# Attention of eight pairs of heads: the second half of two pairs instead of three is computed last, and the last output row block ends in a piece of 128 columns

## The chip, the cores and the metric

The kernel runs on one core of a Trainium2 chip. The engines are TensorE (PE, with its weight loads as PEld), VectorE (DVE), ScalarE (ACT), GpSimd (POOL) and SyncE (SP, here only a DMA queue). The metric is the device time of one execution in microseconds. Before the change three runs took 1085.05, 1080.59 and 1086.14 us (median 1085.05), and the profiled execution took 1081.32 us, of which 1078.8 us are the span that the profile shows.

## The reference

A decoder trunk of two layers runs on one sequence of 1024 tokens of width 1024. The even layer mixes an RWKV-7 and a gated MLP part; the change does not touch it. The odd layer is sliding-window attention and takes the last third of the time:

```
# odd layer, 16 heads of 64, 2 key/value heads, window 128, blocks of 128 queries
h  = modulate(rmsnorm(x), c)                 # adaLN
q, k, v, z = split(h @ W_in)
S  = -(q k^T)/8 + alibi                      # a block sees itself and the block before
P  = softmax with one learned sink per head
o  = P @ v
y  = o * silu(z)
x  = x + gate(c) * (y @ W_out)
out = rmsnorm(x)                             # the final norm
```

## The kernel before

Tokens are split into two halves of 512 (HT) and eight blocks of 128 (NB); heads go in eight pairs, n = 0 to 7 (KC = 8). A product of float32 matrices is made of three matmuls on a high and a low part of each side (hi·hi, hi·lo, lo·hi); a projection of 512 tokens is 24 matmuls of 512 columns into a PSUM tile `pproj`, of which there are two.

For each pair, `head_projs(n)` projects the queries (`qproj`, L1365: two casts on ACT, L1373, and two on DVE, L1374) and the gate z (`zgate`, L1358: tanh on ACT, L1362, and the product on DVE, L1363, into `y`). Pairs 0 to 5 project both halves there; for pairs 6 and 7 the second halves come last, at the end of `head_projs(7)`, in the order q of 7, z of 7, q of 6, z of 6.

`attend(n, half, Q, bias)` runs four iterations, one for each block of 128 queries. An iteration has four score matmuls (`pS`, L130), the bias and minimum on DVE (L1320), the exponentials on ACT (L1324), the reciprocal (DVE L1326), a fold of the two windows (POOL L1329), the scaling (ACT L1331), two transposes (PE L1334, `pT`), the high part (ACT L1337, `PH`) and low part (DVE L1338, `PL`) of the transposed probabilities, a causal mask on each (L1341: POOL for PH, DVE for PL), and four matmuls with the values (`po`). For every two iterations ACT (L1351, L1352) and DVE (L1353, L1354) combine the heads, and POOL multiplies into `y` (L1356).

The loop over pairs attends both halves of a pair for n < N1 (5), and only the first half for the others. After the loop, the second halves that were kept follow in the order 5, 7, 6. The program puts attention at a high priority, and a scheduler at build time then lays out one fixed order for each engine; the engines run their orders by themselves and wait for each other by semaphores. The queries of the kept second halves live in buffers of their own (tag QL, six of them), the others in tag Q (seven), which later holds the rows `gate` and `xr` too.

`wo_load(n)` (L1392) brings one half of the output weight's columns in eight chunks: a DMA on SP into one of three buffers `wraw` (L1398), the high part on ACT (`hi`, L1399), the low part on POOL or DVE in turn (`lo`, L1400). The first half is loaded before the last four projections, the second after the loop.

The tail adds the gate rows (`gate` + `gateb`, DVE L1439, both brought by DMAs on ACT's queue, L1433), and then for each block of 128 tokens splits y (`yh` ACT L1445, `yl` DVE L1446), multiplies by the weight in pieces of 512 columns (24 matmuls each into `pproj`), multiplies by the gate (DVE L1458), adds x (DVE L1459), squares and sums (ACT L1460), and after all pieces takes the root on POOL (L1466) and scales and writes the rows (L1469 to L1474). The last block has three pieces, `cuts`, and multiplies by the final norm's factor (L1462) piece by piece.

Of the kernel before, what the change touches and what calls it, by code (L numbers as in the profile page):

```python
# [11 lines left out]
F32 = mybir.dt.float32  # L12
# [8 lines left out]
P = 128  # L21
D = 1024
T = 1024
KC = 8
HT = 512
NB = 8
# [79 lines left out]
def tile_kernel(ctx, tc, x, cons, par, rows, ada, ada0, ew, wup, sgw, sgb, ewo, ow, owo, out, dbg=None):  # L106
# [25 lines left out]
    def transpose(out, in_, ident):  # L132
        clock[0] += 512 / 2400.0
        return nc.tensor.transpose(out, in_, ident)  # L134
# [131 lines left out]
    def proj(w, h, half):  # L266
        whi, wlo = w
        hhi, hlo = h[half]
        pt = pproj("pproj")
        for k in range(KC):  # L270
            mm(pt, lhsT=whi[:, k, :], rhs=hhi[:, k, :], start=(k == 0), stop=False)
            mm(pt, lhsT=whi[:, k, :], rhs=hlo[:, k, :], start=False, stop=False)
            mm(pt, lhsT=wlo[:, k, :], rhs=hhi[:, k, :], start=False, stop=(k == KC - 1))
        return pt
# [260 lines left out]
    gated = dp.tile([2, D], F32, name="gated")  # L535
# [565 lines left out]
    x1d = dp.tile([T, D], F32, name="x1d")  # L1101
# [142 lines left out]
    def p1(tag):  # L1244
        return ps.tile([P, HT], F32, name="p" + tag, tag=tag, bufs=2)
# [4 lines left out]
    at = ctx.enter_context(tc.tile_pool(name="at", bufs=1, side="right", reuse_waits="tile"))  # L1250
# [9 lines left out]
    for half in range(2):  # L1260
        sl = slice(half * HT, (half + 1) * HT)
# [13 lines left out]
    for half in range(2):  # L1275
        vt = at.tile([P, HT], F32, name="vt", tag="zth", bufs=2)
        S.activation(vt, proj(done["w9"], h, half) if half else done["v0"], AF.Copy, scale=0.5)  # L1277
        pt = p1("T")
        for i in range(4):
            transpose(pt[:, i * P:(i + 1) * P], vt[:, i * P:(i + 1) * P], ident)  # L1280
        p5 = pt.rearrange("p (b g d) -> p b g d", b=4, g=2)
        vb = slice(half * 4, half * 4 + 4 - half)
        for g in range(2):
            S.activation(VV[:, vb, g, 0, :], p5[:, 0:4 - half, g, :], AF.Copy)
            V.tensor_tensor(out=VV[:, vb, g, 1, :], in0=p5[:, 0:4 - half, g, :], in1=VV[:, vb, g, 0, :].bitcast(F32), op=ALU.subtract)
        vf = at.tile([P, 4, 2, 64], F32, name="vf", tag="QL", bufs=2 * (KC - 5))
        S.activation(vf, p5, AF.Copy)
        vfs.append(vf)
        dv = at.tile([P, 4, 2, 64], F32, name="dv", tag="QL", bufs=2 * (KC - 5))
        V.tensor_tensor(out=dv[:, 1:4], in0=p5[:, 1:4], in1=vf[:, 0:3], op=ALU.subtract)  # L1290
        i0 = 1 - half
        if half:
            V.tensor_tensor(out=dv[:, 0], in0=p5[:, 0], in1=vfs[0][:, 3], op=ALU.subtract)
        db = slice(half * 4 - 1 + i0, half * 4 + 3)
        S.activation(DV[:, db, :, 0, :], dv[:, i0:4], AF.Copy)
        G.tensor_tensor(out=DV[:, db, :, 1, :], in0=dv[:, i0:4], in1=DV[:, db, :, 0, :].bitcast(F32), op=ALU.subtract)

    N1 = 5

    def attend(n, half, Q, bias):  # L1300
        g = n // 4
# [63 lines left out]
    def qproj(n, w, half):  # L1365
        pt = proj(w, h, half)
        Q = []
        for e in range(2):
            a = slice(e * 64, e * 64 + 64)
            o = slice(64 - e * 64, 128 - e * 64)  # L1370
            tag, bufs = ("QL", 2 * (KC - N1)) if half and n >= N1 else ("Q", 7)
            q = at.tile([P, HT], F32R, name="Q", tag=tag, bufs=bufs)
            S.activation(q[a, :], pt[a, :], AF.Copy, scale=-0.125)  # L1373
            V.scalar_tensor_tensor(out=q[o, :], in0=pt[a, :], scalar=-0.125, in1=q[a, :].bitcast(F32), op0=ALU.mult, op1=ALU.subtract)  # L1374
            Q.append(q)
        qs[n, half] = Q
# [36 lines left out]
    for n in range(KC):  # L1413
        bias = biases(n)
        for half in range(2 if n < N1 else 1):
            with tc.high_priority(offset=BOOST):
# [4 lines left out]
    wo_load(1)  # L1421
    for n in (*range(N1, KC - 2), KC - 1, KC - 2):
        with tc.high_priority(offset=BOOST):
# [6 lines left out]
    def half_tiles(name, tag, bufs, src, dt=F32):  # L1430
        ts = [at.tile([P, HT], dt, name=name, tag=tag, bufs=bufs) for n in range(2)]
        for n in range(2):
            nc.scalar.dma_start(out=ts[n], in_=src(slice(n * HT, (n + 1) * HT)))  # L1433
        return ts

    gate = half_tiles("gate", "Q", 7, lambda ns: gated[1, ns].partition_broadcast(P))
    gb = half_tiles("gateb", "zth", 2, lambda ns: rows[1, ns].partition_broadcast(P))
    for n in range(2):
        V.tensor_tensor(out=gate[n], in0=gate[n], in1=gb[n], op=ALU.add)  # L1439
# [1 line left out]
    for b in range(NB):  # L1441
        sl = slice(b * P, (b + 1) * P)
# [1 line left out]
        yl = wp.tile([P, KC, P], F32R, name="yl", tag="wlo", bufs=2)  # L1444
        S.activation(yh, y[:, :, sl], AF.Copy)  # L1445
        V.tensor_tensor(out=yl, in0=y[:, :, sl], in1=yh.bitcast(F32), op=ALU.subtract)  # L1446
        xt = half_tiles("xr", "Q", 7, lambda ns: x1d[sl, ns])
        st = at.tile([P, 4], F32, name="st", tag="st", bufs=4)
        cuts = (0, HT, D) if b < NB - 1 else (0, HT, HT + 256, D)
        for i, (c0, c1) in enumerate(zip(cuts, cuts[1:])):  # L1450
            wh, wl = (w[:, :, c0 % HT:c0 % HT + c1 - c0] for w in wo[c0 // HT])
            xs_ = xt[c0 // HT][:, c0 % HT:c0 % HT + c1 - c0]
# [77 lines left out]
```

## Time and profile before

| what | us |
|---|---|
| median of three runs | 1085.05 |
| profiled execution | 1081.32 |
| its span | 1078.8 |
| odd layer's projections, from about | 738 |
| last projection's last matmul starts | 968.66 |
| first matmul of the output product | 974.20 |
| last matmul of the output product starts | 1071.52 |

In a row of the timeline stand the start, the length, engine, line, operation, output and inputs, and in brackets how long the engine was idle before it and what ended that. In a row of a group, behind the first bar, stand the busy time of all its instructions and the mean of one in ns, then the idle time before them. Starts of pipelined matmuls are the better clock: a matmul's length overlaps the next one.

### The profile page before, as it was taken

The page shows a single profiled execution, that of the slowest core. Times are in us where ns is not written, and L with a number is a line of the kernel's source. Part 1 is how long each engine was busy: PE and PEld are TensorE (multiplying, and loading weights), DVE is VectorE, ACT ScalarE, POOL GpSimd, SP SyncE. Part 2 cuts the span into 40 slices and gives each one's busy share as a digit, 9 for nine tenths or more (in the row PEclk, how much of TensorE's full clock was granted, in tenths as well). Part 3 has the DMA queues.
Part 4 walks back from the last instruction along what each step waited for, and adds up shares of the span by engine and source line. Part 5 has one row for each costly group of instructions (what it writes and reads, how often), then busy time and mean ns, then how long its engine had stood idle before and what let it go on. Part 6 is the DMA issues. An engine that isn't in the chain of part 4 may idle for free.

```text
span 1078.8 us, 20631 instructions
## 1 busy us (share of the span) xinstructions
PE 1031.4 (96%) x7776; PEld 824.6 (76%) x7776; DVE 714.6 (66%) x1727; ACT 551.8 (51%) x1383; POOL 405.5 (38%) x471
## 2 busy tenths in 40 slices
PE   6989999998999899999999999999999999999997
PEld 3657777777777777777888777878888888887886
DVE  4354948685868686867533588865767775688744
ACT  4464454545454646453514223336877786797221
POOL 2343323222333324232425100135666676688201
PEclk9999989999999999999999999999999999998999
DMA  9601221212132112121314454421110111332221
GB/s 363 241 18 39 65 74 40 81 49 69 52 99 67 60 50 80 57 71 58 107 47 154 146 181 152 165 77 40 40 40 21 40 40 39 120 111 84 101 95 69
DMA packets 55852, 94.53 MB, mean 88 GB/s; under 512 B 5829, under 2 KB 16197, under 8 KB 55753
## 3 DMA queue, kind: packets, MB, share of 16 engines
q1 hardware_dynamic: 45752, 78.41, 22.0%
q10 hardware_dynamic: 10000, 14.81, 4.5%
q8 instruction: 61, 1.00, 0.4%
q14 instruction: 39, 0.31, 0.1%
HBM read 80.61 MB, written 12.59 MB: 86 GB/s over the span
## 4 chain that ended last, share of the span: by engine, by line
PE 49%; DVE 4%; DMA 3%; ACT 2%; issue 1%; POOL 0%; POOLq 0%; ACTq 0%; DVEq 0%; SPq 0%
PE pproj L130 25%; PE op L130 14%; PE pS L130 2%; PE po L130 2%; PE pT L1334 1%; DMA araw<-ada 1%; DMA wraw<-owo 1%; PE htp L134 1%; PE pM L130 1%; DVE pr L728 1%; PE py L130 0%; DMA wraw<-y0d 0%; DVE adacc L944 0%; PE mix L130 0%; PE mq L130 0%
## 5 line engine op out<-in xcount | busy, mean ns | idle before, releaser
L130 PE MATMUL pproj<-hi,whi 128*128 128x512 f32 x696 | 282.5, 406 | 0.7 <-ACT vt L1277 0.7
L130 PE MATMUL pproj<-lo,whi 128*128 128x512 f32 x696 | 281.4, 404 | 0.0
L130 PE MATMUL pproj<-hi,wlo 128*128 128x512 f32 x696 | 281.3, 404 | 0.0
L258 POOL TENSOR_TENSOR wlo<-wraw,whi 128x512 fp32r<-128x512 f32 x90 | 121.2, 1364 | 145.5 <-ACT whi L257 145.4
L130 PEld LDWEIGHTS pproj<-hi,whi 128*128 128x128 f32 x696 | 131.8, 189 | 28.2 <-issue 4.0
L130 PEld LDWEIGHTS pproj<-hi,wlo 128*128 128x128 f32 x696 | 131.7, 189 | 26.4 <-issue 2.4
L130 PEld LDWEIGHTS pproj<-lo,whi 128*128 128x128 f32 x696 | 132.1, 190 | 25.2 <-issue 1.7
L130 PE MATMUL op<-wo,whi 128*128 128x512 f32 x256 | 81.1, 397 | 0.1
L257 ACT ACTIVATE whi<-wraw 128x512 fp32r<-128x512 f32 x106 | 61.3, 622 | 25.6 <-PE pproj L130 12.4
L1324 ACT ACTIVATE Sx<-Sx,nm 128x257 f32<-128x257 f32 (+1 forms) x128 | 62.1, 488 | 12.7 <-DVE nm L1320 12.3
L1320 DVE CUSTOM_DVE_ANT_0 Sx<-pS,bias,nsink 128x256 f32<-128x256 f32 (+1 forms) x128 | 53.1, 462 | 17.1 <-PE pS L130 14.2
L944 DVE SCALAR_TENSOR_TENSOR adacc<-araw,cond,adacc 128x512 f32<-128x512 f32 x56 | 48.3, 862 | 19.6 <-DMA araw<-ada 19.2
L130 PEld LDWEIGHTS op<-wo,whi 128*128 128x128 f32 x256 | 47.6, 188 | 11.3 <-ACT whi L257 0.5
L130 PE MATMUL op<-hi,yh 128*128 128x512 f32 (+1 forms) x136 | 52.4, 385 | 1.2 <-DVE y L1363 1.2
L1341 POOL TENSOR_TENSOR PH<-PH,causal 128x256 fp32r<-128x256 f32 x56 | 46.1, 825 | 18.9 <-ACT PH L1337 18.5
L130 PE MATMUL op<-hi,yl 128*128 128x512 f32 (+1 forms) x136 | 52.4, 385 | 0.0
L130 PE MATMUL op<-lo,yh 128*128 128x512 f32 (+1 forms) x136 | 52.3, 384 | 0.0
L130 PE MATMUL op<-wo,wlo 128*128 128x512 f32 x128 | 50.8, 397 | 0.0
L1331 ACT ACTIVATE Sx<-Sx,rc 128x128 f32<-128x128 f32 x128 | 43.7, 393 | 5.8 <-POOL Sx L1329 4.6
L1329 POOL TENSOR_TENSOR Sx<-Sx 128x256 f32<-128x256 f32 x56 | 42.2, 755 | 11.4 <-ACT Sx L1324 10.7
L225 POOL TENSOR_TENSOR st<-st,nhalf 128x1 f32<-128x1 f32 x16 | 9.6, 601 | 97.1 <-DVE st L224 97.1
L728 DVE TENSOR_TENSOR pr<-Lf,LT 128x2 f32<-128x2 f32 (+14 forms) x120 | 42.3, 353 | 2.4
(329 smaller groups left out, 2242.7 us busy)
## 6 DMA issues: line engine op xcount, KB each, us to landing
araw<-ada SPq DMA_DIRECT2D x64, 256.0 KB, 2.7
wraw<-ew SPq DMA_DIRECT2D x50, 256.0 KB, 3.0
wraw<-ow SPq DMA_DIRECT2D x40, 256.0 KB, 2.7
adaraw<-ada SPq DMA_DIRECT2D x16, 512.0 KB, 8.3
x<-x SPq DMA_DIRECT2D x8, 512.0 KB, 9.2
woraw<-ewo SPq DMA_DIRECT2D x16, 256.0 KB, 3.0
xr<-x ACTq DMA_DIRECT2D x16, 256.0 KB, 3.6
wraw<-y0d SPq DMA_DIRECT2D x16, 256.0 KB, 3.6
```

The lines of the kernel that those rows point to most:

```text
L130: last[0] = nc.tensor.matmul(out, lhsT=lhsT, rhs=rhs, **kw).ins
L134: return nc.tensor.transpose(out, in_, ident)
L257: a = S.activation(hi[:, gs, :], raws[g], AF.Copy)
L258: b = E.tensor_tensor(out=lo[:, gs, :], in0=raws[g], in1=hi[:, gs, :].bitcast(F32), op=ALU.subtract)
L728: V.tensor_tensor(out=pr[:, 0:nc_, 0:i + 1], in0=Lf[:, i:i + 1, 0:i + 1].to_broadcast([P, nc_, i + 1]), in1=LTt[:, 0:nc_, 0:i + 1], op=ALU ...
L944: op = V.scalar_tensor_tensor(out=acc, in0=raw, scalar=cond[:, k:k + 1], in1=acc, op0=ALU.mult, op1=ALU.add)
L1320: V.tensor_tensor_reduce(out=Sx[:, e, off:2 * P], in0=pS3[:, e, 0:nk], in1=bias[e][:, off:], scale=1.0, scalar=nsink[:, hd:hd + 1], op0=AL ...
L1324: S.activation(pr[:, e, off:2 * P + 1], Sx[:, e, off:2 * P + 1], AF.Exp, bias=nm[:, e:e + 1], scale=-1.0, accum_out=sm[:, e:e + 1])
L1329: G.tensor_tensor(out=F, in0=F, in1=pr[:, :, P:2 * P], op=ALU.add)
L1331: S.activation(F[:, e, :], F[:, e, :], AF.Copy, scale=rc[:, e:e + 1])
L1334: nc.tensor.transpose(pT[:, e * P:(e + 1) * P], F[:, e, :], ident)
L1341: E.tensor_tensor(out=pp_[:, 1, :].rearrange("p (e q) -> p e q", e=2), in0=pp_[:, 0, :].bitcast(F32).rearrange("p (e q) -> p e q", e=2), i ...
```

## The change

N1 goes from 5 to 6: pair 5's second half is attended in the loop and no longer kept, so two pairs (7, then 6) follow after the loop. Its queries take buffers of tag Q, which has one more, and tag QL has two fewer. In the last block of the tail, the three pieces are 512, 384 and 128 columns instead of 512, 256 and 256.

```diff
--- before.py
+++ after.py
@@ -1283,10 +1283,10 @@
         for g in range(2):
             S.activation(VV[:, vb, g, 0, :], p5[:, 0:4 - half, g, :], AF.Copy)
             V.tensor_tensor(out=VV[:, vb, g, 1, :], in0=p5[:, 0:4 - half, g, :], in1=VV[:, vb, g, 0, :].bitcast(F32), op=ALU.subtract)
-        vf = at.tile([P, 4, 2, 64], F32, name="vf", tag="QL", bufs=2 * (KC - 5))
+        vf = at.tile([P, 4, 2, 64], F32, name="vf", tag="QL", bufs=2 * (KC - 6))
         S.activation(vf, p5, AF.Copy)
         vfs.append(vf)
-        dv = at.tile([P, 4, 2, 64], F32, name="dv", tag="QL", bufs=2 * (KC - 5))
+        dv = at.tile([P, 4, 2, 64], F32, name="dv", tag="QL", bufs=2 * (KC - 6))
         V.tensor_tensor(out=dv[:, 1:4], in0=p5[:, 1:4], in1=vf[:, 0:3], op=ALU.subtract)
         i0 = 1 - half
         if half:
@@ -1295,7 +1295,7 @@
         S.activation(DV[:, db, :, 0, :], dv[:, i0:4], AF.Copy)
         G.tensor_tensor(out=DV[:, db, :, 1, :], in0=dv[:, i0:4], in1=DV[:, db, :, 0, :].bitcast(F32), op=ALU.subtract)
 
-    N1 = 5
+    N1 = 6
 
     def attend(n, half, Q, bias):
         g = n // 4
@@ -1368,7 +1368,7 @@
         for e in range(2):
             a = slice(e * 64, e * 64 + 64)
             o = slice(64 - e * 64, 128 - e * 64)
-            tag, bufs = ("QL", 2 * (KC - N1)) if half and n >= N1 else ("Q", 7)
+            tag, bufs = ("QL", 2 * (KC - N1)) if half and n >= N1 else ("Q", 8)
             q = at.tile([P, HT], F32R, name="Q", tag=tag, bufs=bufs)
             S.activation(q[a, :], pt[a, :], AF.Copy, scale=-0.125)
             V.scalar_tensor_tensor(out=q[o, :], in0=pt[a, :], scalar=-0.125, in1=q[a, :].bitcast(F32), op0=ALU.mult, op1=ALU.subtract)
@@ -1433,7 +1433,7 @@
             nc.scalar.dma_start(out=ts[n], in_=src(slice(n * HT, (n + 1) * HT)))
         return ts
 
-    gate = half_tiles("gate", "Q", 7, lambda ns: gated[1, ns].partition_broadcast(P))
+    gate = half_tiles("gate", "Q", 8, lambda ns: gated[1, ns].partition_broadcast(P))
     gb = half_tiles("gateb", "zth", 2, lambda ns: rows[1, ns].partition_broadcast(P))
     for n in range(2):
         V.tensor_tensor(out=gate[n], in0=gate[n], in1=gb[n], op=ALU.add)
@@ -1444,9 +1444,9 @@
         yl = wp.tile([P, KC, P], F32R, name="yl", tag="wlo", bufs=2)
         S.activation(yh, y[:, :, sl], AF.Copy)
         V.tensor_tensor(out=yl, in0=y[:, :, sl], in1=yh.bitcast(F32), op=ALU.subtract)
-        xt = half_tiles("xr", "Q", 7, lambda ns: x1d[sl, ns])
+        xt = half_tiles("xr", "Q", 8, lambda ns: x1d[sl, ns])
         st = at.tile([P, 4], F32, name="st", tag="st", bufs=4)
-        cuts = (0, HT, D) if b < NB - 1 else (0, HT, HT + 256, D)
+        cuts = (0, HT, D) if b < NB - 1 else (0, HT, D - P, D)
         for i, (c0, c1) in enumerate(zip(cuts, cuts[1:])):
             wh, wl = (w[:, :, c0 % HT:c0 % HT + c1 - c0] for w in wo[c0 // HT])
             xs_ = xt[c0 // HT][:, c0 % HT:c0 % HT + c1 - c0]
```

The orders of the engines are the same up to the z of pair 5's second half; from there pair 5's blocks 4 to 7 are spread between the last z of pair 5 and the queries of pair 7. SP's order is the same throughout.

On PE, the place where the last projection ends and the output product begins. `pproj` is the projection, `KH_7641` and `KL_7643` are the high and low part of the keys, `op` is the output product's first block. Before, its last rows and the first of the output product:

```order
L130 MATMUL po<-PH,DV 128x256
L1334 MATMUL pT<-con,Sx 128x128 x2
L130 MATMUL pS<-KH_7641,Q 128x256
L130 MATMUL pS<-KL_7643,Q 128x256
L130 MATMUL pS<-KH_7641,Q 128x256
L130 MATMUL pS<-KL_7643,Q 128x256
L130 MATMUL po<-PL,DV 128x256
L130 MATMUL po<-PH,VV 128x256
L1334 MATMUL pT<-con,Sx 128x128 x2
L130 MATMUL po<-PL,VV 128x256
L130 MATMUL po<-PH,DV 128x256
L130 MATMUL op<-hi,yh 128x512
```

The same place now; between the projection's last matmul and the first row stand four score matmuls:

```order
L130 MATMUL po<-PH,VV 128x256
L130 MATMUL po<-PL,VV 128x256
L1334 MATMUL pT<-con,Sx 128x128 x2
L130 MATMUL po<-PH,DV 128x256
L130 MATMUL pS<-KH_7641,Q 128x256
L130 MATMUL pS<-KL_7643,Q 128x256
L130 MATMUL pS<-KH_7641,Q 128x256
L130 MATMUL pS<-KL_7643,Q 128x256
L130 MATMUL op<-hi,yh 128x512
L130 MATMUL op<-lo,yh 128x512
L130 MATMUL op<-hi,yl 128x512
L130 MATMUL op<-hi,yh 128x512
```

Before, the iterations between the two are of pairs 5 and 7 (the fourth block of pair 5's second half and the first ones of pair 7's); now they are of pairs 7 and 6, and of the kept second halves eight iterations are left in all rather than twelve.

On DVE, from the split of y for the first block (`yl`) on. Before:

```order
L1446 TENSOR_TENSOR yl<-y_7630,yh 128x1024
L1338 TENSOR_TENSOR PL<-pT,PH 128x256
L1326 RECIPROCAL rc<-sm 128x2
L1439 TENSOR_TENSOR gate<-gate,gateb 128x512
L1363 SCALAR_TENSOR_TENSOR y_7630<-zth,pproj 128x512
L1341 TENSOR_TENSOR PL<-PL,causal 128x256
L1400 TENSOR_TENSOR lo<-wraw,hi 128x512
```

Now (the rows `Sx,nm` are the scores of pair 6, each with a read of its accumulator):

```order
L1446 TENSOR_TENSOR yl<-y_7630,yh 128x1024
L1320 ISA Sx,nm<-pS,bias,nsink 128x256
L1320 ISA nm 128x1
L1320 ISA Sx,nm<-pS,bias,nsink 128x256
L1320 ISA nm 128x1
L1320 ISA Sx,nm<-pS,bias,nsink 128x256
L1320 ISA nm 128x1
L1320 ISA Sx,nm<-pS,bias,nsink 128x256
L1320 ISA nm 128x1
L1363 SCALAR_TENSOR_TENSOR y_7630<-zth,pproj 128x512
L1439 TENSOR_TENSOR gate<-gate,gateb 128x512
L1400 TENSOR_TENSOR lo<-wraw,hi 128x512
```

The product of the last projection (`y_7630<-zth,pproj`) stood behind the gate sum, and now stands ahead of it; the scores of pair 6 stand between the split and it, and the first remainder of the second half of the weight (`lo`) stands behind both.

On ACT, around the first casts of the weight's second half (`hi<-wraw`) and the DMAs of the gate rows. Before:

```order
L1337 ACTIVATE PH<-pT 128x256
L1433 DMA gateb<-rows 128x512
L1433 DMA fg<-rows 128x512
L1399 ACTIVATE hi<-wraw 128x512
L1433 DMA fg<-rows 128x512
L1399 ACTIVATE hi<-wraw 128x512 x2
L1337 ACTIVATE PH<-pT 128x256
L1399 ACTIVATE hi<-wraw 128x512
L1351 ACTIVATE cm<-po 64x256
```

Now:

```order
L1445 ACTIVATE yh<-y_7630 128x1024
L1362 ACTIVATE zth<-pproj 128x512
L1399 ACTIVATE hi<-wraw 128x512 x3
L1433 DMA gateb<-rows 128x512
L1337 ACTIVATE PH<-pT 128x256
L1324 ACTIVATE Sx,sm<-Sx,nm 128x257 x4
L1337 ACTIVATE PH<-pT 128x256
L1351 ACTIVATE cm<-po 64x256
L1352 ACTIVATE cm<-po 64x256
L1433 DMA gateb<-rows 128x512
L1399 ACTIVATE hi<-wraw 128x512
L1433 DMA fg<-rows 128x512
```

The tanh of the last projection (`zth`) now stands right ahead of the first three casts, the DMAs of `gateb` stand behind these, and from the fourth cast on attention operations stand between the casts.

## The prediction

> **What bounds the kernel now.** I read the busy times first, then the stretches of the last 200 us, then the waits inside the one stretch where TensorE is not busy all the time. The busy times of the page:
>
> ```profile
> PE 1031.4 (96%) x7776; PEld 824.6 (76%) x7776; DVE 714.6 (66%) x1727; ACT 551.8 (51%) x1383; POOL 405.5 (38%) x471
> ```
>
> The whole kernel is bound by TensorE (PE); the number of its matmuls hardly changes here, so all that an order can win is idle time or low clock on PE. The table of stretches around the moved work has busy time (and instructions) of PE, weight loads, DVE, ACT and POOL, then the granted clock:
>
> ```profile
> core 0: us, PE busy (x) PEld busy (x) DVE busy (x) ACT busy (x) POOL busy (x), PEclk, DMA share, GB/s
> 880.00:900.00 20.00, 20.00 (x112) 17.21 (x111) 14.70 (x42) 14.78 (x42) 14.96 (x21) 1.00 0.16 53
> 900.00:920.00 20.00, 20.00 (x100) 16.72 (x99) 9.39 (x23) 10.44 (x29) 12.55 (x18) 1.00 0.18 53
> 920.00:940.00 20.00, 20.00 (x108) 17.11 (x107) 11.74 (x40) 14.99 (x47) 11.31 (x16) 1.00 0.38 114
> 940.00:960.00 20.00, 19.41 (x112) 16.64 (x111) 18.04 (x56) 18.29 (x55) 17.47 (x26) 1.00 0.42 139
> 960.00:980.00 20.00, 17.57 (x80) 14.14 (x79) 14.92 (x35) 16.94 (x48) 15.82 (x21) 0.83 0.34 101
> 969.05:972.47 3.42, 2.14 (x15) 1.54 (x14) 2.80 (x6) 3.42 (x9) 2.12 (x4) 1.00 0.33 77
> 972.47:979.29 6.82, 5.66 (x16) 4.30 (x15) 4.92 (x8) 4.48 (x12) 5.89 (x6) 0.50 0.49 150
> ```
>
> From 880 to 940 us PE never idles and the other engines have room. From 940 to 980 they are nearly full, and PE idles 20 - 19.41 = 0.59 and 20 - 17.57 = 2.43 us, 3.0 together. From 972.47 to 979.29 the granted clock is 0.50: 5.66 us busy did 2.8 us of full-speed work and lost **2.8 us**. So some 5.9 us lie here. These are PE's waits there:
>
> ```profile
> 954.23 0.39 PE L130 MATMUL pS<-KH,Q 128*128 128x256 f32 x1 [0.22 <-DVE Q L1374]
> ...
> 968.66 0.40 PE L130 MATMUL pproj<-hi,wlo 128*128 128x512 f32 x1
> ...
> 969.81 0.39 PE L130 MATMUL pS<-KH,Q 128*128 128x256 f32 x1 [0.19 <-DVE Q L1374]
> ...
> 972.20 0.42 PE L1334 MATMUL pT<-con,Sx 128*128 128x128 f32 x2 [1.09 <-DVE rc L1326]
> ...
> 974.20 0.80 PE L130 MATMUL op<-hi,yh 128*128 128x512 f32 x1 [1.16 <-DVE y L1363]
> ```
>
> The row at 968.66 is the last matmul of the last projection (z, pair 6, second half). After it PE has only attention to do and then waits at 972.20 and 974.20. Why so late is on DVE:
>
> ```profile
> 970.49 1.23 DVE L1446 TENSOR_TENSOR yl<-y,yh 128x1024 fp32r<-128x1024 f32 x1 [0.21 <-issue]
> ...
> 972.49 1.07 DVE L1439 TENSOR_TENSOR gate<-gate,gateb 128x512 f32<-128x512 f32 x1 [0.36 <-DMA gateb<-rows]
> ...
> 973.48 0.67 DVE L1363 SCALAR_TENSOR_TENSOR y<-zth,pproj 128x512 f32<-128x512 f32 x1
> ...
> 988.42 1.14 DVE L1400 TENSOR_TENSOR lo<-wraw,hi 128x512 fp32r<-128x512 f32 x1
> ```
>
> The output product needs the PSUM buffer that L1363 empties, and L1363 stands behind the gate sum, which waits for a DMA. The attention's transpose at 972.20 stands behind the same queue: the 1.23-us split of y holds DVE ahead of it.
>
> **What the moved half removes.** Pair 5's four iterations leave the end and go among the projections from about 890 to 935 us. Their load, per iteration, from the groups of the odd layer (an iteration has two L1324, its read, two L1331, one L1337, and one of L1351/L1352; on POOL one of L1341 and L1329 and half of L1356):
>
> ```profile
> L1324 ACT ACTIVATE Sx<-Sx,nm 128x257 f32<-128x257 f32 (+1 forms) x128 | 62.1, 488 | 12.7 <-DVE nm L1320 12.3
> ...
> L1324 ACT ACTIVATION_READ_ACCUMULATOR Sx<-Sx,nm 128x1 f32 x128 | 24.2, 189 | 0.0
> ...
> L1331 ACT ACTIVATE Sx<-Sx,rc 128x128 f32<-128x128 f32 x128 | 43.7, 393 | 5.8 <-POOL Sx L1329 4.6 <-DVE rc L1326 0.7
> ...
> L1337 ACT ACTIVATE PH<-pT 128x256 fp32r<-128x256 f32 x64 | 23.8, 374 | 9.6 <-PE po L130 7.4 <-PE pT L1334 1.6
> ...
> L1351 ACT ACTIVATE cm<-po 64x256 f32<-64x256 f32 x32 | 12.1, 380 | 11.6 <-PE po L130 6.8 <-DMA out<-xr 4.3
> ...
> L1341 POOL TENSOR_TENSOR PH<-PH,causal 128x256 fp32r<-128x256 f32 x56 | 46.1, 825 | 18.9 <-ACT PH L1337 18.5
> ...
> L1329 POOL TENSOR_TENSOR Sx<-Sx 128x256 f32<-128x256 f32 x56 | 42.2, 755 | 11.4 <-ACT Sx L1324 10.7
> ...
> L1356 POOL TENSOR_TENSOR y<-y,cm 128x256 f32<-128x256 f32 x32 | 25.7, 804 | 12.3 <-DVE cm L1354 12.1
> ```
>
> ACT: 2 x (0.488 + 0.189) + 2 x 0.393 + 0.374 + 0.38 = 2.9 us, four times 11.6. POOL: 0.825 + 0.755 + 0.40 = 2.0, four times 7.9. With what lies there from 880 to 940, ACT comes to 14.78 + 10.44 + 14.99 + 11.6 = 51.8 of 60 us (86%) and POOL to 46.7 (78%). The nearest stretch as full, 940 to 960 with ACT at 91%, cost PE 0.59 us in 20; so the new place costs between nothing and 1.8 us. I take 0, as from 880 to 900 three engines at 73 to 75% cost nothing; if this cover fails, matmuls of the projections queue behind the waiting scores. At the end, the same four iterations no longer stand on ACT, DVE and POOL. In the new order DVE has L1363 ahead of the gate sum, so the wait of 1.16 us has no queue, and the transpose no longer comes right behind the 1.23-us split. An iteration issues no DMA, SP's order stays as it was, and the buffers only change hands (eight of Q for seven, four of QL for six): nothing for these. I count the whole stretch as gone: **-5.9 us** (no more is to be had from 940 to 980; at the least -2.3, the two waits of 1.09 and 1.16 alone).
>
> **What takes its place.** First, pair 7's scores now come sooner behind their projection and need both casts of Q; the two rows of 0.2 us above are the same wait: **+0.5** (0 to 1). Second, the larger one: PE gets to the second piece of the output product sooner. Its weights (second half of columns) come in 8 chunks through 3 raw buffers: DMA, cast on ACT (L1399), remainder on POOL or DVE (L1400).
>
> ```profile
> 971.53 1.67 ACT L1399 ACTIVATE hi<-wraw 128x512 fp32r<-128x512 f32 x3
> ...
> 978.71 0.63 ACT L1399 ACTIVATE hi<-wraw 128x512 fp32r<-128x512 f32 x1 [2.26 <-DMA wraw<-owo]
> ...
> 994.00 0.39 PE L130 MATMUL op<-hi,yl 128*128 128x512 f32 x1
> ...
> DMA to landing us min/median/max: 2.6/3.6/4.8
> ```
>
> The first cast starts at 971.53 and the last remainder ends at 988.42 + 1.14 = 989.56: 18.0 us. Now PE reaches the last chunk about 993.3 (three matmuls up to the row at 994.00), so nobody waits. In the new order, by counts of matmuls at 0.227 us for 512 columns and 0.118 for 256 (the starts above are 0.23 and 0.12 apart), PE has 45 matmuls of the output product (10.2 us) and 43 of attention (5.1 us), 15.3 us, from the end of the last projection to that chunk. ACT starts the first cast right behind that projection's tanh, 0.8 us after its end, so the chain would end at 0.8 + 18.0 = 18.8: **a new wait of 3.5 us** (between 0, if the casts follow the DMAs at the median 3.6 us for each three chunks, and 5.5, if DVE's remainders stay behind the gate sum, which waits for its DMA as it did 1.82 us in this row):
>
> ```profile
> 978.90 0.69 DVE L1439 TENSOR_TENSOR gate<-gate,gateb 128x512 f32<-128x512 f32 x1 [1.82 <-DMA gateb<-rows]
> ```
>
> In-order PE has nothing to put into it: the attention's matmuls queue behind the waiting one.
>
> **The last piece.** 256 + 256 columns become 384 + 128. Prices:
>
> ```profile
> 738.21 0.22 PE L130 MATMUL pS<-KH,Q 128*128 128x128 f32 x1
> ...
> 739.13 0.40 PE L130 MATMUL pproj<-hi,whi 128*128 128x512 f32 x1
> ...
> 1071.40 0.28 PE L130 MATMUL op<-lo,yh 128*128 128x256 f32 x1
> ...
> 1071.52 0.28 PE L130 MATMUL op<-hi,yl 128*128 128x256 f32 x1
> ...
> 1071.83 0.43 DVE L1458 TENSOR_TENSOR op<-op,gate 128x256 f32<-128x256 f32 x1 [1.20 <-PE op L130]
> ...
> L1458 DVE TENSOR_TENSOR op<-op,gate 128x512 f32<-128x512 f32 x5 | 3.5, 700 | 9.6 <-PE op L130 9.6
> ```
>
> Between the first two rows lie four matmuls of 128 and four of 256 columns: (0.92 - 4 x 0.118)/4 = 0.112 us for 128. The 384 lies between 0.12 and 0.227: 0.173. So 24 x 0.112 + 24 x 0.173 - 48 x 0.12 = +1.1 us on PE. Behind the last matmul, DVE's two operations shrink by (0.700 - 0.43)/2 = 0.13 each, and the square and the last product on 128 columns alike: -0.5. **Net +0.6.** If 128 columns cost half of 256 (0.06) it is -0.7; if as much as 512, +3.3. The Trainium skill, "TensorE: Matmul & The Clock Gate", section "Back-to-back issue gap", gives about 81 ns for a sustained matmul of 128 columns with its weight load; by that the net would be -0.2. The row above gives 0.112, and no row here shows 81 ns.
>
> **The sum** for the profiled execution (span 1078.8, with what lies around it 1081.32 us): -5.9 + 0.5 + 3.5 + 0.6 = -1.3, so 1080.0. The other runs are 1080.59, 1085.05 and 1086.14; the four have a mean of 1083.3, 2.0 above the profiled one. I add that: **1082.0**.
>
> **Rivals.**
>
> (a) *The chunks come in time*: no new wait. For it: three chunks per 3.6-us landing would end well inside 15 us. Against: the casts took 18.0 us before. -5.9 + 0.5 + 0.6 = -4.8: 1078.5. With a cheap last piece (-0.7) and no wait for Q, -6.6: 1076.7, or 1074.7 without the 2.0 for the other runs.
>
> (b) *Slower*: the chunks come later still, and PE's clock falls again. It decides when the last remainder ends over 4 us behind PE's arrival, 19.3 us after the last projection. For it: the half clock from 972.47 came behind a window in which PE was busy 2.14 of 3.42 us, with single waits of 1.1 at most, and a wait of 4 to 5.5 us idles more than that. Price: 5.5 + 2.8 for the clock against 3.5: -5.9 + 0.5 + 5.5 + 2.8 + 0.6 = +3.5, 1086.8; with 1.8 for a full ACT earlier, 1088.6. With a wait of 3.5 and the clock's 2.8 it is +1.5, 1084.8. Against it: the wait may come in pieces, a chunk at a time. The Trainium skill's page of that title, section "HAM oscillation — how this bites in real kernels", wants idle gaps of over some 3.4 us before the clock falls. By that rule a wait in pieces would leave the clock whole and 1082.0 would stand. The trace speaks against it: no gap here was over 1.2 us, and the clock fell.
>
> (c) *It does nothing at the end*: y's release and the transpose wait as before, since eight iterations still stand there. For it: DVE's split of y and the DMA behind the gate sum remain. The 5.9 us stay and the new wait doesn't come: +0.6 from the tail, 1083.9.
>
> **How the numbers follow.** The forecast has 0.42, (a) 0.24, (b) 0.24, (c) 0.10. 1082.0 is the forecast's. The range goes from between (a)'s two ends to near (b)'s upper one: 1075.5 to 1088.0. A measurement of this kernel tells about 0.5% (5.4 us) from no change. Faster by that needs (a) with a cheap last piece, or a little more than it: 0.17. Slower needs (b) beyond its price: 0.08. Within: 0.75.
>
> **What would show it.** Right: PE busy without gaps from 940 to 970, no wait of the output product's first matmul on L1363, its second piece waiting for L1399/L1400 for about 3.5 us, and a tail where the 128-column piece takes 2.7 us. (a) would show no such wait; (b) the same wait with a second stretch of clock 0.50. It is wrong if PE waits from 890 to 935 us for ACT or POOL, or if the last piece takes over 3.5 us.

## The result, and the profile after

| | before | changed |
|---|---|---|
| median of 12 runs, us | 1084.66 (1078.31 to 1089.42) | 1079.17 (1075.45 to 1081.72) |
| profiled execution, us (span) | 1081.32 (1078.8) | 1079.72 (1077.9) |
| mean granted clock of the profiled execution | 0.984 | 0.984 |

The ratio of changed to before is 0.9949, with a 95% interval of 0.993 to 0.9968. That is 5.5 us by the medians, at the edge of the 0.5% that was named as the limit of what can be told. The forecast was 1082.0, 1075.5 to 1088.0.

The two spans differ by only 0.9 us, so the pair of profiles seems to contradict the medians. The first thing to do is to cut off what the change can't have touched. From the first cast of the odd layer's V product (L1277), before which nothing moved, to the end of the span, the profile of before has 364.12 us and that of the changed kernel 361.42: 2.7 us less. What lies ahead of that cast happened to take 1.8 us more. So this pair shows 2.7 us, the runs 5.5. Both numbers have to be explained.

The stretches of the changed kernel, with the same columns as those of before:

```profile
core 0: us, PE busy (x) PEld busy (x) DVE busy (x) ACT busy (x) POOL busy (x), PEclk, DMA share, GB/s
880.00:900.00 20.00, 20.00 (x112) 17.15 (x111) 14.71 (x43) 14.17 (x41) 15.54 (x23) 1.00 0.11 38
900.00:920.00 20.00, 20.00 (x112) 17.18 (x112) 13.56 (x46) 16.78 (x54) 13.40 (x22) 1.00 0.14 42
920.00:940.00 20.00, 20.00 (x111) 17.20 (x109) 13.63 (x40) 14.88 (x44) 14.20 (x21) 1.00 0.19 60
940.00:960.00 20.00, 18.75 (x107) 16.10 (x106) 14.96 (x40) 16.69 (x47) 15.20 (x21) 1.00 0.62 206
960.00:980.00 20.00, 20.00 (x109) 17.15 (x108) 16.96 (x47) 18.43 (x54) 15.75 (x21) 1.00 0.26 82
980.00:1000.00 20.00, 19.21 (x97) 15.31 (x96) 18.91 (x46) 12.85 (x35) 13.53 (x15) 1.00 0.36 118
```

From 880 to 940 us PE still never idles, though ACT now has 45.8 of 60 us instead of 40.2: the new place of pair 5's second half was free. (The prediction put 51.8 there. The exponentials, L1324, run 28 times in it instead of 22, so about three of the four moved iterations fell into this stretch, and its other work on ACT became less.) The granted clock is 1.00 throughout. PE idles 1.25 us from 940 to 960, none from 960 to 980, and 0.79 from 980 to 1000, where it idled not at all before.

PE's rows of the changed kernel at those places, and the first matmul of the output product:

```profile
957.93 0.38 PE L130 MATMUL po<-PL,VV 128*128 128x256 f32 x1 [0.75 <-DVE PL L1338]
959.41 0.38 PE L130 MATMUL po<-PH,VV 128*128 128x256 f32 x1 [0.50 <-ACT PH L1337]
973.11 0.40 PE L130 MATMUL pproj<-hi,wlo 128*128 128x512 f32 x1
974.86 0.39 PE L130 MATMUL op<-hi,yh 128*128 128x512 f32 x1
988.09 0.50 PE L130 MATMUL op<-lo,yh 128*128 128x512 f32 x1 [0.73 <-DVE lo L1400]
991.74 0.40 PE L130 MATMUL op<-hi,yl 128*128 128x512 f32 x1
```

The first output matmul comes 1.75 us behind the last projection's last one, and waits for nothing; before it was 974.20 - 968.66 = 5.54 us, of which some 2.0 us were matmuls. A new wait of 1.25 us stands among the last projections, where DVE and ACT work on the chunks of the first weight half. And the second piece of the output product waits for the weight's remainders, as forecast: from the first output matmul to the last one of that piece (991.74) it is 16.9 us, while by the count of the new order 14.6 us would do. That is a wait of 2.3 us, spread over three chunks and, in between, over two parts of attention (`PL` and `Sx`). Before, the last projection's last matmul and the last one of that piece were 22.6 us apart, now 18.6; by the prices of the prediction both orders have 16.4 us of matmuls in between. So 6.2 us beyond the matmuls became 2.3.

### The profile page after: what moved, and what is told of

It reads as the page before. It is cut to its first block, busy times and chain, and to the rows that moved or that the text cites. A ratio compares the mean times of both kernels' runs of the same rounds, so it can differ in the third digit from the quotient of the medians.

```text
span 1077.9 us, 20631 instructions
## 1 busy us (share of the span) xinstructions
PE 1032.5 (96%) x7776; PEld 825.9 (77%) x7776; DVE 712.5 (66%) x1727; ACT 552.4 (51%) x1383; POOL 402.1 (37%) x469
## 4 chain that ended last, share of the span: by engine, by line
PE 52%; DVE 3%; ACT 2%; issue 1%; POOL 1%; DMA 1%; POOLq 0%; ACTq 0%; SPq 0%; DVEq 0%
PE pproj L130 25%; PE op L130 16%; PE pS L130 3%; PE po L130 3%; PE pT L1334 1%; PE htp L134 1%; DVE pr L728 1%; PE pM L130 1%; PE py L130 0%; DMA wraw<-y0d 0%; PE mix L130 0%; PE mq L130 0%; PE gvn L130 0%; PE uw L130 0%; ACT Dg L710 0%
## 5 line engine op out<-in xcount | busy, mean ns | idle before, releaser
L1324 ACT ACTIVATE Sx<-Sx,nm 128x257 f32<-128x257 f32 (+1 forms) x128 | 62.1, 488 | 11.9 <-DVE nm L1320 11.5
L130 PE MATMUL op<-lo,yh 128*128 128x512 f32 (+2 forms) x136 | 51.9, 381 | 0.7 <-DVE lo L1400 0.7
L130 PE MATMUL op<-hi,yh 128*128 128x512 f32 (+2 forms) x136 | 51.8, 381 | 0.0
L130 PE MATMUL op<-hi,yl 128*128 128x512 f32 (+2 forms) x136 | 51.6, 380 | 0.0
L1341 POOL TENSOR_TENSOR PH<-PH,causal 128x256 fp32r<-128x256 f32 x56 | 44.5, 796 | 14.6 <-ACT PH L1337 14.4
```

Of the source, the lines that this page charges most:

```text
L130: last[0] = nc.tensor.matmul(out, lhsT=lhsT, rhs=rhs, **kw).ins
L1324: S.activation(pr[:, e, off:2 * P + 1], Sx[:, e, off:2 * P + 1], AF.Exp, bias=nm[:, e:e + 1], scale=-1.0, accum_out=sm[:, e:e + 1])
L1341: E.tensor_tensor(out=pp_[:, 1, :].rearrange("p (e q) -> p e q", e=2), in0=pp_[:, 0, :].bitcast(F32).rearrange("p (e q) -> p e q", e=2), i ...
```

## The experiments

All the lengths below that are called "odd layer" run from the first cast of V (L1277) to the end of the span, or, where the text says so, to the start of the last block's gate product of its first 512 columns, which leaves out the changed tail. They are given against the first profile of before.

**The same kernel again.** A copy of the kernel before gives its own spread.

> The kernel before once more, unchanged, for its own spread of granted clock. Theory 'end stretch' (the loss lies in the waits and the half clock where the projections end, and its size changes from run to run with the clock's windows): the mean granted clock of the runs is lower than that of the changed kernel's runs (0.982 to 0.991), by about 0.002 (half clock of 2.5 us in some runs and 5 in others), and the profiled run shows a granted clock under 1.00 somewhere from 960 to 985 us. Rival 'chance' (the profiled pair's 2.7 us are all, the rest is the scatter of the even layer): the clocks have the same mean and the ratio to the kernel before is 1.000.

Measured: 1083.93 us, ratio 0.9977 (0.9955 to 0.9999). An identical kernel can thus come out 0.2% off; no difference of that size is read into anything below. The odd layer was 4.2 us longer than in the first profile, of one and the same program. The mean clock of its 12 runs is 0.9832, of the changed kernel's 12 runs 0.9859, a little more apart than the 0.002 of the first theory. The copy's stretches and PE's two large waits:

```profile
955.00:960.00 5.00, 4.78 (x17) 3.91 (x17) 4.39 (x14) 4.94 (x18) 4.74 (x7) 0.66 0.16 54
...
970.00:975.00 5.00, 3.61 (x24) 2.98 (x22) 3.74 (x12) 4.41 (x11) 3.64 (x6) 1.00 0.14 52
975.00:980.00 5.00, 2.69 (x6) 2.16 (x7) 4.97 (x6) 3.86 (x11) 4.94 (x5) 0.63 0.48 144
980.00:985.00 5.00, 5.00 (x18) 4.00 (x17) 2.99 (x7) 1.26 (x2) 2.49 (x2) 0.69 0.64 220
```

```profile
974.08 0.41 PE L1334 MATMUL pT<-con,Sx 128*128 128x128 f32 x2 [1.11 <-DVE rc L1326]
977.31 0.80 PE L130 MATMUL op<-hi,yh 128*128 128x512 f32 x1 [2.58 <-DVE y L1363]
```

The wait for the transposes is the same 1.1 us, that for L1363 has grown from 1.16 to 2.58, and the clock fell twice instead of once: at 955 to 960 us and at 975 to 985 us. But most of the 4.2 us is lost earlier: matmul by matmul, the copy is 1.8 us behind the first profile at 952.6 us, 3.4 at the last projection's last matmul, and 3.9 at the first output matmul.

**The two halves of the change, one by one.** The move alone, with the old pieces of the last block:

```diff
-        cuts = (0, HT, D) if b < NB - 1 else (0, HT, D - P, D)
+        cuts = (0, HT, D) if b < NB - 1 else (0, HT, HT + 256, D)
```

> Pair 5's second half moved as in the change, the last block in pieces of 512, 256, 256 as before. 'End stretch': all of the gain is here, and the piece of 128 costs 0.7 us, so this is 0.5 to 1 us faster than the changed kernel: about 0.994 to 0.995 of before, 1078.5 us. In the trace the odd layer up to the last 1024 columns is 3.3 us shorter than before. Rival 'tail' (the shorter chain behind the last matmul brings the gain): 0.998 to 1.000 of before, 1083 us or more.

Measured: 1077.33 us, ratio 0.9927 (0.9898 to 0.9955). The odd layer is 3.23 us shorter up to the last block and still 3.23 at the end. So the move brings all of the gain.

The pieces alone, on the kernel before:

```diff
-        cuts = (0, HT, D) if b < NB - 1 else (0, HT, HT + 256, D)
+        cuts = (0, HT, D) if b < NB - 1 else (0, HT, D - P, D)
```

> Only the last block's pieces changed (512, 384, 128), five pairs in the loop as before. 'End stretch': +1.06 us on TensorE and -0.4 behind it, +0.7 us in the trace, 1.0005 of before in time, within the scatter of the runs. Rival 'tail': 2 to 5 us faster, ratio 0.995 to 0.998. The wait of 1.1 us for DVE at the last projection's end and the first output matmul's 1.2 us are as before under both.

Measured: 1084.80 us, ratio 0.9999 (0.9976 to 1.0022). In the trace, the odd layer was 3.72 us longer than in the first profile up to the last block, which is the loss of the run before once more (the same waits of 1.11 and 2.58 us, the clock down at 955 to 960 and 975 to 985), and 4.28 at the end: the pieces cost 0.56 us. In the changed kernel they cost 3.35 - 2.69 = 0.66.

**Only the order of two rows on DVE.** In the kernel before, the gate sum is ordered behind the last projection's product (a dependency for the scheduler, no semaphore):

```diff
+        yops.append(V.scalar_tensor_tensor(out=y[:, n, sl], in0=th, scalar=1.0, in1=pt, op0=ALU.add, op1=ALU.mult).ins)
...
-        V.tensor_tensor(out=gate[n], in0=gate[n], in1=gb[n], op=ALU.add)
+        behind(V.tensor_tensor(out=gate[n], in0=gate[n], in1=gb[n], op=ALU.add), yops[-1])
```

> Five pairs in the loop and the old pieces, but the gate sum on DVE is ordered behind the last projection's product (L1363); the order of TensorE is the same up to the first 19 matmuls of the output product. Theory 'the order on DVE' (the gate sum, waiting for its DMA ahead of that product, makes the stop and with it the half clock): the wait of 1.16 us at the first output matmul falls to 0.5 or less, the granted clock stays at 1.00 there, and 3 to 4 us of the gain come without moving any attention: ratio 0.996 to 0.997. Theory 'load' (the engines are too full with twelve iterations at the end): the transposes still wait 1.1 us and another wait takes the place, the clock falls as before, ratio 0.999 to 1.000.

Measured: 1081.35 us, ratio 0.9965 (0.9944 to 0.9985). PE's waits for DVE and ACT in the odd layer of this run:

```profile
PE pT L1334 <- DVE rc L1326: 1.1, 1, 1.1
PE pS L130 <- DVE nm L1320: 0.8, 2, 0.4
PE po L130 <- ACT PH L1337: 0.4, 1, 0.4
PE po L130 <- DVE PL L1341: 0.4, 1, 0.4
...
```

The wait for L1363 is gone, the clock is 1.00 from 940 to 1000 us, and the ratio lies where the first theory had it. The ratio alone proves little, since the copy's was 0.9977: by their means the two sets of 12 runs differ by 2.1 us, with an interval that includes 0. Half of it holds for the second theory: the transposes' 1.1 us stay. The odd layer is 0.79 us shorter than in the first profile of before, but 5.0 shorter than in the copy's. Of these 5.0, 1.7 are won ahead of the two rows, where the copy's clock fell and this one's didn't, and 2.6 at the first output matmul. And it loses ground behind the first output matmul: 0.36 us ahead there, 1.39 ahead at the first gate product (L1458), 1.41 behind at the third, 0.79 ahead at the end. The order alone doesn't get what the move gets (1081.35 against 1077.33 us).

**The same two rows put back in the kernel with the move.**

```diff
...
+        gop = V.tensor_tensor(out=gate[n], in0=gate[n], in1=gb[n], op=ALU.add)
+        if n == 0:
+            behind(yops[-1], gop.ins)
```

> As the kernel with the moved half and the old pieces, but the last projection's product on DVE is ordered behind the gate sum again, as before the change; two rows of DVE change places, and TensorE's order is the same. Theory 'buffer' (with the move, the first output product got the PSUM buffer that the casts of Q empty, and the product's buffer is needed only at the second piece, 6.7 us later): no wait at the first output matmul, the time within 0.2% of the kernel without the swap, ratio 0.992 to 0.995, odd layer 3 us shorter than before. Theory 'order on DVE' (the two rows alone decide): a wait of 1 to 2.6 us comes back there, the clock falls to half behind it in the trace, and 3 to 5 us are lost: ratio 0.996 to 0.998.

Measured: 1076.58 us, ratio 0.9932 (0.9909 to 0.9954); odd layer 3.37 us shorter. DVE's two rows (the edit moves the lines behind it by two, so the gate sum is L1441), and PE's around the first output matmul:

```profile
975.19 1.43 DVE L1441 TENSOR_TENSOR gate<-gate,gateb 128x512 f32<-128x512 f32 x1
976.54 0.68 DVE L1363 SCALAR_TENSOR_TENSOR y<-zth,pproj 128x512 f32<-128x512 f32 x1
```

```profile
972.15 0.28 PE L130 MATMUL pS<-KL,Q 128*128 128x256 f32 x1
972.26 0.39 PE L130 MATMUL op<-hi,yh 128*128 128x512 f32 x1
```

The output product had begun 4.3 us before L1363 did, and waited for nothing. So the order on DVE decides only in the kernel before. The times say why. There are two `pproj` buffers in PSUM, and at the end the queries of pair 6 lie in one and the last projection (z of pair 6) in the other; each is free when DVE has read it for the last time, in the second cast (L1374) or in L1363. The last cast of the kernel before, then that cast and L1363 of the changed kernel:

```profile
975.93 0.69 DVE L1374 SCALAR_TENSOR_TENSOR Q<-pproj,Q 64x512 fp32r<-64x512 f32 x1
```

```profile
972.95 0.69 DVE L1374 SCALAR_TENSOR_TENSOR Q<-pproj,Q 64x512 fp32r<-64x512 f32 x1
...
977.78 0.69 DVE L1363 SCALAR_TENSOR_TENSOR y<-zth,pproj 128x512 f32<-128x512 f32 x1
```

Before, the output product began at 974.20, ahead of the cast, so it can only have taken the buffer of z. In the changed kernel it began at 974.86, behind the cast and ahead of L1363, so it took that of the queries. That the scheduler chose by which of the two it expected to be free first is likely, but not shown.

**How the loss varies.** Two more profiles of the kernel before and two of the changed one, each with nothing altered.

> The kernel before, one more profile. Theory 'varying loss' (the half clock and the wait for the gate rows' DMA change from execution to execution): from the odd layer's start to the last matmul it is 2 to 5 us longer than in the first profile in most executions, with granted clock under 1.00 in one or two stretches from 950 to 985 us. Rival 'chance in two profiles': it is within 0.5 us of the first profile.

> As the run before it: 2 to 5 us longer in the odd layer than the first profile under 'varying loss', within 0.5 us under the rival.

> The changed kernel, one more profile. Under 'varying loss' its waits are too short to bring the clock down: granted clock 1.00 from 940 to 1060 us and the odd layer within 0.7 us of the first profile of the changed kernel. Rival: it has a half clock too in some executions, 2.5 us longer or more.

> As the run before it: clock 1.00 and within 0.7 us under 'varying loss', 2.5 us longer or more under the rival.

Measured, with the earlier profiles of the same order (up to the last block's gate product, so that the pieces don't count; "clock down" are the stretches between 940 and 1000 us with a granted clock under 1.00):

| profile | time of its run, us | odd layer against the first of before | clock down |
|---|---|---|---|
| before, first | 1081.32 | 0 | 972 to 979 |
| before, copy | 1084.31 | +4.23 | 955 to 960, 975 to 985 |
| before, with the new pieces | 1086.21 | +3.72 | 955 to 960, 975 to 985 |
| before, third | 1082.19 | -0.47 | none |
| before, fourth | 1085.41 | +4.64 | 955 to 965, 975 to 985 |
| changed, first | 1079.72 | -3.35 | none |
| changed, second | 1079.37 | -2.15 | none |
| changed, third | 1080.11 | -3.12 | none |

One more execution of the kernel before, beside the last four and without a profile, took 1091.42 us. Three of five of the old order lose about 4 us more than the profile on which the prediction was made, none of three of the new one has a clock below 1.00 there. What lies ahead of the first cast of V is no part of it: its mean is 714.9 us in the five and 714.6 in the four profiles of the changed kernel, the one below included.

Where the three begin to lose is on ACT, at a cast of the weight's first half. It stands ahead of a cast of the queries and of attention's work. In the first profile its chunk had landed, in the copy it had not:

```profile
947.03 0.62 ACT L1399 ACTIVATE hi<-wraw 128x512 fp32r<-128x512 f32 x1
```

```profile
947.98 0.63 ACT L1399 ACTIVATE hi<-wraw 128x512 fp32r<-128x512 f32 x1 [1.68 <-DMA wraw<-owo]
```

The other two long executions waited 1.15 and 1.61 us at this cast, the third profile of before not at all. By 952.6 us of the first profile's time PE is 1.3 to 2.6 us behind in the three, and with the half clock that follows it is 2.9 to 5.1 behind at the last projection's last matmul. At the stop of the first output matmul, which all five profiles have, they lose only 1.2 more. So the part of the loss that varies lies mainly here, among the last projections. The run with the two rows exchanged waited 1.60 us at this cast too, and the first three profiles of the changed kernel up to 1.83 us at such casts, and their clock stayed at 1.00. No run changes this DMA alone; that the loss starts with it is read from the order of events.

The third profile of before misses its expectation, and the second of the changed kernel too (1.2 us off the first, not 0.7). The third of before is instructive: it had no half clock at all and yet gained only 0.47 us. Its stretches behind the first output matmul, where the half clock would have been:

```profile
970.00:975.00 5.00, 2.60 (x19) 2.10 (x17) 4.09 (x11) 4.97 (x14) 3.80 (x5) 1.00 0.15 52
975.00:980.00 5.00, 4.94 (x23) 4.13 (x24) 3.58 (x7) 2.88 (x7) 4.24 (x5) 1.00 0.51 159
980.00:985.00 5.00, 5.00 (x31) 4.35 (x30) 3.15 (x6) 2.07 (x4) 3.08 (x3) 1.00 0.60 213
985.00:990.00 5.00, 4.89 (x25) 3.38 (x24) 4.92 (x17) 4.55 (x16) 4.26 (x7) 1.00 0.19 52
```

From 985 to 990 us the weight loads (the second number) fall to 3.38 us: PE came to the second piece sooner (2.96 us ahead at 979.4 us of the first profile's time) and waited there for attention's and the chunks' results instead, 0.47 ahead at the end. In the first profile the half clock had filled that wait.

**What the end hangs on now.** In the changed order the odd layer's end follows one event. From the first cast of V, the last chunk's remainder ended at 274.88, 276.06 and 275.08 us in the three profiles of the changed kernel, at 274.95 with the old pieces and 274.79 with the two rows put back. From there to the last block's gate product it was 73.17, 73.19, 73.20, 73.22 and 73.24 us. In the first profile of before that remainder had ended at 274.88 too, and the gate product came 76.52 us behind it: the move didn't bring the chunk sooner, it brought PE to the chunk sooner, until PE had to wait for it. Two experiments tried to cut this tie. The first gives every fourth chunk a raw buffer of its own, so that four are on the way:

```diff
-            raw = wp.tile([P, HT], F32, name="wraw", tag="wraw", bufs=3)
+            raw = at.tile([P, HT], F32, name="wraw", tag="wx", bufs=1) if n and k % 4 == 3 else wp.tile([P, HT], F32, name="wraw", tag="wraw", bufs=3)
```

> As the kernel with the moved half and the old pieces, but in the second weight load every fourth chunk has a raw buffer of its own, so four chunks are on the way. Theory 'buffers' (the new wait of the output product's second piece, 1.4 us and some weight loads of 0.3, comes from three raw buffers with DMAs of 3 to 4 us): the last chunk's remainder ends about 3 us sooner, the wait is gone, the odd layer is 1 to 2 us shorter: 0.991 of before, 1076 us. Rival 'queues' (the casts and remainders stand behind attention on ACT and DVE): the wait stays at 1 us or more and the odd layer is within 0.4 us.

Measured: 1078.13 us, ratio 0.9954 (0.9933 to 0.9976); odd layer 3.19 us shorter than before, 3.23 without the buffer. The last remainder ended 1.3 us sooner (273.67), not 3, and nothing came of it: PE still waited 1.3 us for one remainder, and its weight loads 0.7 for a low part of attention. That is the rival's result; that it comes from the queues of ACT and DVE is not shown by it.

The second leaves the chunks alone and uses them later: the first two blocks take their first 512 columns, then their last 512.

```diff
...
+    for b in range(2):
+        ss[b] = pre(b)
+        piece(b, ss[b], 0)
+    for b in range(2):
+        piece(b, ss[b], 1)
+        fin(b, ss[b])
...
```

> As the kernel with the moved half and the old pieces, but the first two row blocks take their first 512 columns one after the other, and only then their last 512 columns, so that the second half of the weight is needed 24 matmuls (5.4 us) later. Theory 'last chunk' (in every profile with the moved half the end of the odd layer follows the end of the last chunk's remainder to within 0.1 us; PE has 2.3 us less work ahead of that chunk than the chunk takes): no wait for L1400 on PE, the odd layer's end is no longer tied to that chunk and 1.5 to 2.5 us sooner, 4.7 to 5.7 us shorter than in the first profile of before; ratio 0.990 to 0.991. Rival 'attention' (the remaining eight iterations on DVE and ACT set the end, as when the fourth raw buffer brought the chunk 1.2 us sooner and nothing was won): within 0.5 us of the kernel without it, 3.2 us shorter than before, ratio 0.993.

Measured: 1076.07 us, ratio 0.9940 (0.9920 to 0.9961); odd layer 4.02 us shorter than before up to the last block, so 0.8 more than without it. No wait for L1400 is left, and the last remainder came at 274.71 as ever. The size is between the two theories: the tie to the chunk is cut, but two thirds of the 2.3 us come back as waits for attention. PE's waits in its odd layer:

```profile
PE pT L1334 <- ACT Sx L1331: 0.9, 1, 0.9
PE po L130 <- ACT PH L1337: 0.5, 1, 0.5
PE po L130 <- DVE PL L1338: 0.4, 1, 0.4
```

The changed kernel ran beside it:

> The changed kernel once more beside it: 0.9949 of before as measured, and 0.6 us longer in the last row block than the kernels with the old pieces. The end of its odd layer follows the last chunk's remainder: both later or sooner by the same amount.

Measured: 1076.70 us, ratio 0.9938 (0.9908 to 0.9969). Its last remainder came at 274.80 and its odd layer was 3.40 us shorter up to the last block, 2.74 in all. The kernel with the first pieces first has the shortest odd layer of all, 4.01 us less than before against 2.74 here, of which 0.66 are the last block's pieces; by times the two can't be told apart (their intervals overlap almost wholly).

## Why the prediction was right, and where it was not

The time lies in the range, 2.8 us under the forecast, and the sum went the right way for partly wrong reasons.

**The stretch of 5.9 us: the right place, a wrong reason.** The stop at the first output matmul and the half clock are gone, as forecast. The step "in the new order DVE has L1363 ahead of the gate sum, so the wait of 1.16 us has no queue" is not what did it: with these rows put back, the wait stayed away. It is the PSUM buffer that the output product got. The transposes' wait of 1.09 us did go, too; only the move removed it, the two rows didn't. For the profile from which it was read the size was about right: 6.2 us beyond the matmuls from the last projection to the second piece were there to win, and the new wait of 2.3 is what is left of them. But the 2.8 us of half clock in it weren't a price of their own, as the third profile of before shows: without them PE reached the second piece sooner and waited there.

**The step that failed most: adding the 2.0 us.** The profiled execution was 2.0 us under the mean of the four runs, and the prediction put this on top of the new kernel's time as well. But the excess belongs to the old order: it arises from 947 us on, mostly among the last projections (the late chunk and the half clock behind it), and none of the profiles of the new order shows the half clock there. The four other profiles of the old order lose 3.0 us more on average ((4.23 + 3.72 - 0.47 + 4.64)/4), and the mean of all five is 2.4 over the first; the changed kernel's first three are 2.9 shorter than it up to the tail (3.35, 2.15, 3.12), so 2.9 + 2.4 - 0.66 for the pieces is 4.6 us, near the 5.5 of the medians. The clocks agree: the 69 runs of before beside the experiments have a mean granted clock of 0.9823 and a mean of 1084.3 us, the changed kernel's 20 runs 0.9867 and 1078.1. A difference of 0.0043 over 1080 us is at most 4.7 us of the 6.2; at most, since some of the half clock falls into PE's waits (in the copy, the first 1.05 us of the second fall). These runs come from several chips; on the one that ran both kernels beside each other in the last set, the clocks are 0.9839 and 0.9878.

**The new wait for the chunks: right in kind, half again too large.** Forecast 3.5 us, measured 2.3. The chain's end came out nearly as forecast (18.8 us behind the last projection forecast, 18.2 measured: 274.88 against 256.64 from the first cast of V), but by luck, for two errors cancel. The first cast and the last remainder of the changed kernel:

```profile
975.37 1.67 ACT L1399 ACTIVATE hi<-wraw 128x512 fp32r<-128x512 f32 x3
...
990.66 0.69 DVE L1400 TENSOR_TENSOR lo<-wraw,hi 128x512 fp32r<-128x512 f32 x1
```

The first cast starts 2.3 us behind the start of the last projection's last matmul, not 0.8 behind its end, since on ACT the split of y stands ahead of the tanh; and from there to the last remainder's end it is 16.0 us, not 18.0. The bound of 0 fell, and so did rival (a).

**The wait for Q: wrong name, wrong size.** It was to cost 0.5 us at pair 7's scores. Nobody waited for Q; 1.25 us were lost some rows on, at 957.93 and 959.41, on low and high parts of attention that stand behind casts and chunk work on DVE and ACT. "PE busy without gaps from 940 to 970" was wrong.

**The last piece: right.** Forecast +1.1 on PE and -0.5 behind it, measured +1.06 and -0.40. The profile of the changed kernel:

```profile
1068.33 0.33 PE L130 MATMUL op<-hi,yl 128*128 128x384 f32 x1
1068.50 0.22 PE L130 MATMUL op<-hi,yh 128*128 128x128 f32 x1
...
1071.02 0.28 PE L130 MATMUL op<-hi,yl 128*128 128x128 f32 x1
...
1071.33 0.30 DVE L1458 TENSOR_TENSOR op<-op,gate 128x128 f32<-128x128 f32 x1 [0.58 <-PE op L130]
```

24 matmuls of 128 columns start over 2.52 us, so 0.110 us each (forecast 0.112), and one of 384 takes 0.17. Half the columns saved 8% of the 0.120 us that one of 256 took before. The 81 ns that the Trainium skill gives in "TensorE: Matmul & The Clock Gate", section "Back-to-back issue gap", are not what this product shows.

**Rival (b)** was not seen: the new wait comes in pieces, of which the longest left PE idle for 0.73 us in the first profile and 1.38 in others, and in all eight profiles of kernels with the move the granted clock stays at 1.00 there. **Rival (c)** fell with the first output matmul.

## What to carry to other kernels

Before a sum is made on one profile, ask which of its terms changes from run to run, and put the scatter of the runs on that term, not on both sides: a loss that depends on the clock's state and a DMA's landing is worth its mean. When PE waits for an engine's instruction, look which buffer that instruction frees and whether the order gives the next user another one; moving work can win by the buffer as well as by the queue. And half clock beside waits need not be an extra cost to be added: here one execution without it got only 0.5 us back, since PE then waited for what had not come yet.

## What was not expected of the hardware

The clock fell without any long stop. In the copy of before, the longest waits of PE ahead of the first fall (955.78 us) were these four; at the second fall, at 976.26, PE stood in the wait of 2.58 us.

```profile
952.83 0.38 PE L130 MATMUL po<-PL,DV 128*128 128x256 f32 x1 [0.37 <-DVE PL L1341]
953.64 0.39 PE L130 MATMUL pS<-KH,Q 128*128 128x256 f32 x1 [0.43 <-DVE nm L1320]
...
954.51 0.39 PE L130 MATMUL pS<-KH,Q 128*128 128x256 f32 x1 [0.37 <-DVE nm L1320]
...
955.23 0.38 PE L130 MATMUL pS<-KH,Q 128*128 128x256 f32 x1 [0.22 <-DVE Q L1374]
```

With the same four waits (0.37, 0.42, 0.37, 0.22 us) the run with the two rows exchanged kept its clock at 1.00. The Trainium skill, "TensorE: Matmul & The Clock Gate", section "HAM oscillation — how this bites in real kernels", asks for an idle gap of over some 3.4 us; none of the falls from 940 to 1000 us had one.

The traces show where the two executions differ. In each of the 14 profiles all changes of the granted clock lie whole multiples of 3.41 us apart, so one can lay a grid of 3.41 us through them and read PE's busy time in each of its windows. In the copy all four waits lie in one window, from 952.37 to 955.78 us, with PE busy for 2.02 of 3.41 us, and the clock falls at its end. In the run with the two rows exchanged the grid cuts between them: 2.73 and 2.59 us busy, and no fall. From 720 to 1060 us there are seven falls in the 14 profiles, each behind a window with PE busy for at most 0.63 of it (0.63 in the first profile of before, 0.59 in the copy at the first fall and 0.22 at the second). No window above 0.63 has a fall behind it; two of about 0.6 have none either, one of them in the new order (with the old pieces). So each fall has such a window ahead of it, but the share by this profile doesn't decide it alone; what else does is open, and the new order may not be safe from it.
